# A decoder step on one core: small first loads, one prepared unit ahead and products of ones at the beginning

## The chip, the cores and the metric

The kernel runs on one core of one Trainium2 chip. Its time is the device time of one execution in microseconds (us). Five engines work side by side, each through its own list of instructions in order: TensorE (PE, products and transposes), VectorE (DVE), ScalarE (ACT), GpSimd (POOL) and SyncE (SP, which here only issues DMAs). An instruction waits on semaphores for what it reads, and everything behind it on the same engine waits too.

## The reference

One layer of a hybrid decoder for 256 prompt tokens and 64 sample tokens. The change touches its first stage alone, keys and values of 256 memory tokens:

```python
def mem_kv(mem, g, wk, wv):
    mn = rmsnorm(mem, g)                     # (256, 2048)
    k = (mn @ wk).reshape(b, 256, 4, 512)    # 2048 x 2048 weights
    v = (mn @ wv).reshape(b, 256, 4, 512)
```

Behind it come the mixer (RMSNorm of the tokens, W_in, state space and short convolution, W_out), attention over the memory and a layer of 16384 single-neuron experts, all in float32.

## The kernel before

A float32 product is made of three products in a reduced format: each operand x is split into a high part H (ACT, line 248) and a rest L = x - H (DVE, line 249), and the sum of a-high by H, a-high by L and a-low by H is accumulated.

The stage works in **units**. For each of w_mem_k and w_mem_v and each of four blocks c of 512 columns there are 16 units k, one for each 128 rows of weights: 128 units in all. A unit has a load (one DMA of two units' weights, 512 KB, into one of four rooms `W`), a preparation (`prep`: the split into H and L) and its products (`comp`: six products of 128x512, lines 318 to 320, three for each half of the memory tokens). The units of the first block take their first rooms from `w0`.

The memory rows come as two tiles of 128 tokens x 2048 (`mem`, printed `xt`). The generator `mem_in` makes the stationary operands: one step transposes two 128-column pieces of both tiles on PE (four transposes, line 241, into `pt`), and ACT and DVE scale them by the norm gain and split them into `MH` and `ML` (`scaled_split`, lines 281 and 282), for the units k = 2g and 2g + 1. After eight such steps two more square the rows for the norm's scale (line 459), which is applied when a block leaves PSUM.

`Stream` orders all this at build time. `add` issues a unit's load at once and holds three units back; `prepare` takes the next, emits the preparation of the unit before it (`late`) and puts the new one in a queue; when more than `room["g"]` units (GD = 6) are queued, `pop` emits the oldest one's products. With each pop, side generators advance at their rates: `mem_in` 0.75 steps a unit, and the chain of `x_norm` (norm and transposes of the layer's tokens), `vectors` (norm and convolution weights) and `histories` (convolution states) 0.3. PE, ACT and DVE run in the order that is written; SP and POOL are ordered by a scheduler.

Of the kernel before, what the change touches and what calls it, by code (L numbers as in the profile page):

```python
# [19 lines left out]
P = 128  # L20
# [23 lines left out]
HLB, GD, WA, WB = 7, 6, 3, 4  # L44
# [105 lines left out]
def wait(n):  # L150
    for _ in range(n):
        yield 1
# [11 lines left out]
def step(ctx, tc, ins, outs, dbg=None, stop=None):  # L164
    nc = tc.nc
# [22 lines left out]
    def ps(name="ps"):  # L188
        return psp.tile([P, 512], F32, tag="ps", name=name)

    V, S, G, PE = nc.vector, nc.scalar, nc.gpsimd, nc.tensor
# [6 lines left out]
    ones = cst.tile([P, P], F32, tag="ones", bufs=1, name="ones")  # L198
# [9 lines left out]
    def wtile(beside=None):  # L208

        r = min((r for r in range(len(rooms)) if rooms[r][1] is None),  # L210
                key=lambda r: (rooms[r ^ 1][1] is not beside, rooms[r][2]))
        rooms[r][1] = rooms[r][0]
        return rooms[r][0]
# [12 lines left out]
    def wfree(w):  # L226
        for r in rooms:
            if r[1] is w:
                r[1:] = None, next(turn)
# [3 lines left out]
    def high():  # L233
        return wp.tile([P, 512], F32R, tag="H", bufs=HLB, name="H")

    def low():
        return wp.tile([P, 512], F32R, tag="L", bufs=HLB, name="L")

    def transpose(out, in_):
        n = in_.shape[0]  # L240
        PE.transpose(out, in_, ident[:n, :n])


    strm = Stream(WA, g=GD, a=2)

    def split(h, l, src):

        S.activation(h, src, AF.Copy)  # L248
        V.tensor_tensor(l, src, h.bitcast(F32), ALU.subtract)  # L249
# [37 lines left out]
    def tokens_gemm(w2d, c, ah, al, evac, w0=None):  # L287

        pts, box = [], {}

        def unit(k):
            def load():
                if k % 2 == 0:
                    if w0 is not None and k < 4:
                        w = w0[k // 2]
                    else:
                        w = wtile()
                        nc.sync.dma_start(w.rearrange("p (k n) -> p k n", n=512),
                                          w2d[k * P:(k + 2) * P, 512 * c:512 * c + 512].rearrange("(k p) n -> p k n", p=P))
                    box["room", k + 1] = box["w"] = w  # L300
                box["w", k] = box["w"][:, 512 * (k % 2):512 * (k % 2) + 512]

            def prep():
                h, l = high(), low()
                split(h, l, box.pop(("w", k)))
                if k % 2:
                    wfree(box.pop(("room", k)))
                box[k] = h, l
                if w0 is not None and k == 0:
                    next(mi)  # L310

            def comp():
                if k == 0:
                    pts.extend(ps(f"pg{m}") for m in range(2))
                h, l = box.pop(k)
                for m in range(2):
                    a0, a1 = ah[:, k, m * P:(m + 1) * P], al[:, k, m * P:(m + 1) * P]
                    PE.matmul(pts[m], a0, h, start=k == 0, stop=False)
                    PE.matmul(pts[m], a0, l, start=False, stop=False)
                    PE.matmul(pts[m], a1, h, start=False, stop=k == KC - 1)  # L320
                if k == KC - 1:
                    for m in range(2):
                        evac(m, pts[m])

            strm.add(load, None, prep, comp)

        for k in range(KC):
            unit(k)
# [93 lines left out]
    def norm_T(src, n, gb, h, l, cols):  # L422

        xt = tokens()
        nc.sync.dma_start(xt[:n], src)
        yield from wait(2)
        V.scalar_tensor_tensor(xt[:n], xt[:n], stats(xt, n), gb[:n], ALU.mult, ALU.mult)
        yield from wait(2)
        for g in range(4):
            pt = ps("pt")  # L430
            for j in range(4):
                k = 4 * g + j
                transpose(pt[:, j * n:(j + 1) * n], xt[:n, k * P:(k + 1) * P])
            split(h[:, 4 * g:4 * g + 4, cols], l[:, 4 * g:4 * g + 4, cols],
                  pt[:, 0:4 * n].rearrange("p (j n) -> p j n", j=4))
            yield 1

    def gain_rows(g):
        gb = pM.tile([P, D], F32, tag="gb", bufs=1, name="gb")
        nc.sync.dma_start(gb, g.rearrange("(o d) -> o d", o=1).broadcast_to([P, D]))  # L440
        return gb
# [3 lines left out]
    nc.sync.dma_start(gk, norm_mem_kv[0].rearrange("(k p) -> k p", p=P))  # L445
    mem = [tokens() for _ in range(2)]
    w0 = [wtile()]
    w0.append(wtile(w0[0]))

    for i, (c0, c1) in enumerate(((0, 512), (512, 1024), (1024, 2048))):  # L450
        for b in range(2):
            nc.sync.dma_start(mem[b][:, c0:c1], mem_prompt[0, b * P:(b + 1) * P, c0:c1])
        if i < 2:
            nc.sync.dma_start(w0[i], w_mem_k[0, 256 * i:256 * i + 256, 0:512].rearrange("(k p) n -> p k n", p=P))
    squares = [pM.tile([P, 4], F32, name=f"sq{b}") for b in range(2)]

    def half_square(b, i):
# [2 lines left out]

    S.activation(squares[0][:, 0:1], ones[:, 0:1], AF.Sqrt)
    pk = ps("pk")
    transpose(pk[:, 0:16], gk)
    V.tensor_copy(GAIN[:, 48:64], pk[:, 0:16])
    mem_scale = []

    def mem_in():
        for g in range(8):
            pt = ps("pt")
            for j in range(2):  # L470
                for b in range(2):
                    transpose(pt[:, (2 * j + b) * P:(2 * j + b + 1) * P], mem[b][:, (2 * g + j) * P:(2 * g + j + 1) * P])
            for j in range(2):
                k = 2 * g + j
                scaled_split(MH[:, k], ML[:, k], pt[:, j * TP:(j + 1) * TP], gain(3, k))
            yield 1
        for b in range(2):
            half_square(b, 0)
            half_square(b, 1)
            sq = squares[b]  # L480
            V.tensor_tensor(sq[:, 0:1], sq[:, 0:1], sq[:, 1:2], ALU.add)
            mem_scale.append(rstd(sq, P))
            yield 1

    mi = mem_in()
    next(mi)
    strm.side(mi, 0.75)

    def x_norm():
        gb = gain_rows(norm_mix[0])  # L490
        yield from wait(2)
        for b in range(2):
            yield from norm_T(x_prompt[0, b * P:(b + 1) * P], P, gb, AH, AL, slice(b * P, b * P + P))
        yield from norm_T(x_sample.rearrange("b l d -> (b l) d"), TS, gb, AH, AL, slice(TP, T))
# [77 lines left out]

    strm.steady = chain(wait(136), ordered_rows(0.272))
    side = strm.side(chain(x_norm(), vectors(), histories()), 0.3)
    for w, dst in ((w_mem_k, p_mem_k), (w_mem_v, p_mem_v)):
        d2 = dst[0, 0].rearrange("m h d -> m (h d)")
        for c in range(4):
            def evac(m, pt, c=c, d2=d2):
                o = pM.tile([P, 512], F32, tag="kvo", bufs=2, name="kvo")
                S.activation(o, pt, AF.Copy, scale=mem_scale[m])  # L580
                nc.gpsimd.dma_start(d2[m * P:m * P + P, 512 * c:512 * c + 512], o)
# [1634 lines left out]
```

## Time and profile before

| | us |
|---|---|
| time, median of three runs (lowest, highest) | 3133.64 (3127.72, 3135.29) |
| the profiled execution: its time | 3134.84 |
| the profiled execution: span from first to last instruction | 3133.1 |
| TensorE busy | 3072.1 (98%) |
| VectorE, ScalarE, GpSimd busy | 2281.8, 1594.7, 1343.9 |
| first product of unit 0 starts | 8.80 |
| first product of the next stage (W_in) starts | 206.16 |

Busy time says how long an engine had an instruction in work. The rows by time give the start, the time in work, engine, line, operation, written and read tiles, and in brackets how long the engine sat idle before and what released it. PE's products overlap, so the distance between their starts is their price.

### The profile page before, as it was taken

Reading aid. Unit: us, or ns where it says so; the run is one execution under the profiler, and the core shown is the slowest. Engines: PE = TensorE matmul, PEld = TensorE weight load, DVE = VectorE, ACT = ScalarE, POOL = GpSimd, SP = SyncE. Lnnn points to the kernel's source line nnn. Section 1 sums busy time; section 2 is a strip of 40 time slices with the busy share of each in tenths; the row PEclk is TensorE's granted clock in tenths of the full one; section 3 lists DMA queues with packets and bytes.
Section 4 is the critical chain, followed back from the end, with each engine's and each line's share of the span. In section 5 each row is a group of like instructions: output and inputs, shape, how many; then the busy total and the mean of one; then the engine's idle time right before and its main releaser. Section 6 shows DMA issues by size and latency. Waiting matters only on the chain. (4 is left out here: it accounts for less than half of the span.)

```text
span 3133.1 us, 55416 instructions
## 1 busy us (share of the span) xinstructions
PE 3072.1 (98%) x19749; PEld 2806.7 (90%) x19749; DVE 2281.8 (73%) x4482; ACT 1594.7 (51%) x3207; POOL 1343.9 (43%) x1490
## 2 busy tenths in 40 slices
PE   8999999999999998999999999999999999999997
PEld 7889999999999998779999999888888888878886
DVE  5556766666566456556787899988885888878886
ACT  5545544334554443334454444776675555545555
POOL 0012221111100012320348999989886656456553
PEclk9999999999999999999999999999999999999999
DMA  7668899899999999984866788879998999899996
GB/s 259 210 194 299 307 325 322 308 326 311 335 322 309 314 292 241 252 263 145 228 212 216 274 318 306 314 280 327 329 337 263 340 345 362 314 324 332 327 320 200
DMA packets 442177, 909.15 MB, mean 290 GB/s; under 512 B 39679, under 2 KB 248743, under 8 KB 416388
## 3 DMA queue, kind: packets, MB, share of 16 engines
q1 hardware_dynamic: 313804, 544.07, 51.1%
q0 software_dynamic: 60512, 227.32, 22.3%
q10 hardware_dynamic: 67584, 134.23, 12.4%
q8 instruction: 154, 2.52, 0.3%
q14 instruction: 123, 1.01, 0.1%
HBM read 849.41 MB, written 190.05 MB: 332 GB/s over the span
## 5 line engine op out<-in xcount | busy, mean ns | idle before, releaser
L249 DVE TENSOR_TENSOR L<-W,H 128x512 fp32r<-128x512 f32 x1320 | 903.5, 709 | 390.2 <-ACT H L248 377.3
L248 ACT ACTIVATE H<-W 128x512 fp32r<-128x512 f32 x1320 | 797.4, 625 | 694.9 <-PE acc L2119 216.0
L1924 POOL TENSOR_TENSOR L<-tt,H 128x512 fp32r<-128x512 f32 x509 | 645.0, 1299 | 63.7 <-ACT H L1921 55.9
L371 PE MATMUL pg<-AH,H 128*128 128x320 f32 (+1 forms) x1872 | 587.6, 314 | 0.0
L373 PE MATMUL pg<-AH,L 128*128 128x320 f32 (+1 forms) x1872 | 578.8, 309 | 0.0
L372 PE MATMUL pg<-AL,H 128*128 128x320 f32 (+1 forms) x1872 | 578.4, 309 | 0.0
L2118 PE MATMUL acc<-L,wt 128*128 128x512 f32 x1024 | 399.9, 390 | 4.0 <-DVE L L249 4.0
L2117 PE MATMUL acc<-H,wt 128*128 128x512 f32 x1024 | 399.4, 390 | 2.9 <-DVE at L1957 2.9
L2119 PE MATMUL acc<-H,wt 128*128 128x512 f32 x1024 | 399.5, 390 | 0.0
L1912 DVE STREAM_TRANSPOSE tt<-W 128x512 f32<-128x512 f32 x512 | 337.0, 690 | 59.9 <-POOL L L1924 57.4
L1943 PE MATMUL pu<-XP,H 128*128 128x512 f32 x1050 | 376.8, 399 | 0.0
L1921 ACT ACTIVATE H<-tt 128x512 fp32r<-128x512 f32 x512 | 306.7, 625 | 134.0 <-DVE tt L1912 105.0
L371 PEld LDWEIGHTS pg<-AH,H 128*128 128x128 f32 (+1 forms) x1872 | 350.9, 187 | 2.4 <-issue 0.2
L372 PEld LDWEIGHTS pg<-AL,H 128*128 128x128 f32 (+1 forms) x1872 | 350.6, 187 | 2.2
L373 PEld LDWEIGHTS pg<-AH,L 128*128 128x128 f32 (+1 forms) x1872 | 350.4, 187 | 0.6
L1944 PE MATMUL pu<-XP,L 128*128 128x256 f32 x1120 | 301.5, 279 | 0.1
L2066 POOL TENSOR_TENSOR at<-at,G 128x108 f32<-128x108 f32 x192 | 161.4, 854 | 262.8 <-DMA at<-act_d 228.5
L1950 PE MATMUL pu<-XP,L 128*128 128x256 f32 x928 | 263.8, 284 | 3.7 <-POOL L L1924 3.5
L1948 PE MATMUL pu<-XP,H 128*128 128x256 f32 x928 | 263.2, 284 | 0.0
L1949 PE MATMUL pu<-XP,H 128*128 128x256 f32 x928 | 262.5, 283 | 0.0
L2118 PEld LDWEIGHTS acc<-L,wt 128*128 128x128 f32 x1024 | 192.9, 188 | 45.2 <-DVE L L249 5.0
L1943 PEld LDWEIGHTS pu<-XP,H 128*128 128x128 f32 x1050 | 197.1, 188 | 40.3
(496 smaller groups left out, 5822.0 us busy)
## 6 DMA issues: line engine op xcount, KB each, us to landing
u_d<-in_peer_u_dram ACTq DMA_DIRECT2D x128, 1024.0 KB
W<-u_d SPq DMA_DIRECT2D x128, 1024.0 KB
W<-in_peer_v_dram SPq DMA_DIRECT2D x256, 512.0 KB
W<-in_w_in_dram SPq DMA_DIRECT2D x176, 512.0 KB
W<-in_w_out_dram SPq DMA_DIRECT2D x64, 512.0 KB
W<-in_w_mem_k_dram SPq DMA_DIRECT2D x32, 512.0 KB
W<-in_w_mem_v_dram SPq DMA_DIRECT2D x32, 512.0 KB
W<-in_w_mem_q_dram SPq DMA_DIRECT2D x32, 512.0 KB
```

Source lines behind the costliest of these rows:

```text
L248: S.activation(h, src, AF.Copy)
L249: V.tensor_tensor(l, src, h.bitcast(F32), ALU.subtract)
L371: PE.matmul(out, hv[:, j, c0:c1], ah[:, k, 0:n], start=st, stop=False)
L372: PE.matmul(out, hv[:, j, c0:c1], al[:, k, 0:n], start=False, stop=False)
L373: PE.matmul(out, lv[:, j, c0:c1], ah[:, k, 0:n], start=False, stop=sp)
L1912: V.transpose(tt.rearrange("p (k a i) -> p k a i", a=4, i=32), box["x", i].rearrange("p (a k j) -> p k a j", a=4, k=16)[:, 4 * q:4 * q + 4])
L1921: S.activation(h, src, AF.Copy)
L1924: G.tensor_tensor(l, src, h.bitcast(F32), ALU.subtract)
L1943: PE.matmul(*wide, start=k == 0, stop=False)
L2117: PE.matmul(out, th, h, start=i == 0, stop=False)
L2118: PE.matmul(out, th, l, start=False, stop=False)
L2119: PE.matmul(out, tl, h, start=False, stop=i == P - 1)
```

## The change

The first loads become smaller and alternate: gk, then memory columns 0:256 of both tiles and the weights of units 0 and 1 as two DMAs of 256 KB, then columns 256:768 and units 2 and 3, and so on up to unit 7; all four rooms are `w0` from the start. Until unit 11 has been popped the stream's room is one unit instead of six. `mem_in` is no longer a side generator: its steps are called behind the products of units 0, 2, 4, 6, 8, 10, 11, 13 and 14. Seven products of a tile of ones with itself are put on PE: two before and two after the transpose of gk, three after the first transposes. `x_norm` starts with six more empty steps.

```diff
@@ tokens_gemm
-                    if w0 is not None and k < 4:
+                    if w0 is not None and k < 8:
                         w = w0[k // 2]
...
                 box[k] = h, l
-                if w0 is not None and k == 0:
-                    next(mi)
...
                     PE.matmul(pts[m], a1, h, start=False, stop=k == KC - 1)
+                if w0 is not None:
+                    if k in (0, 2, 4, 6, 8, 10, 11, 13, 14):
+                        next(mi)
+                    if k == 11:
+                        strm.room["g"] = GD
@@ beginning
-    w0.append(wtile(w0[0]))
-
-    for i, (c0, c1) in enumerate(((0, 512), (512, 1024), (1024, 2048))):
+    for i in range(3):
+        w0.append(wtile(w0[-1] if i % 2 == 0 else None))
+
+    for i, (c0, c1) in enumerate(((0, 256), (256, 768), (768, 1408), (1408, 2048))):
         for b in range(2):
             nc.sync.dma_start(mem[b][:, c0:c1], mem_prompt[0, b * P:(b + 1) * P, c0:c1])
-        if i < 2:
-            nc.sync.dma_start(w0[i], w_mem_k[0, 256 * i:256 * i + 256, 0:512].rearrange("(k p) n -> p k n", p=P))
+        for j in range(2):
+            r0 = 256 * i + P * j
+            nc.sync.dma_start(w0[i][:, 512 * j:512 * j + 512], w_mem_k[0, r0:r0 + P, 0:512])
...
+    def warm(n):
+        for _ in range(n):
+            PE.matmul(pk[:, P:2 * P], ones, ones, start=True, stop=True)
+
+    warm(2)
     transpose(pk[:, 0:16], gk)
     V.tensor_copy(GAIN[:, 48:64], pk[:, 0:16])
+    warm(2)
...
     next(mi)
-    strm.side(mi, 0.75)
+    warm(3)
+    strm.room["g"] = 1

     def x_norm():
+        yield from wait(6)
         gb = gain_rows(norm_mix[0])
```

What moves on ACT at the beginning, before (pt_236 is the third group of transposes, H_182 belongs to unit 0, H_195 to unit 1 and so on):

```order
L281 ACTIVATE MH_136<-pt_156,GAIN_77 128x256 x2
L248 ACTIVATE H_182<-W_78 128x512
L281 ACTIVATE MH_136<-pt_186,GAIN_77 128x256 x2
L248 ACTIVATE H_195<-W_78 128x512
L248 ACTIVATE H_200<-W_78 128x512
L248 ACTIVATE H_204<-W_78 128x512
L248 ACTIVATE H_209<-W_78 128x512
L248 ACTIVATE H_213<-W_78 128x512
L248 ACTIVATE H_226<-W_78 128x512
L281 ACTIVATE MH_136<-pt_236,GAIN_77 128x256 x2
L248 ACTIVATE H_245<-W_78 128x512
```

And now (pt_208, pt_237 are the second and third group, H_196 belongs to unit 0, H_217 to unit 1, H_227 to 2, H_246 to 3):

```order
L281 ACTIVATE MH_136<-pt_168,GAIN_77 128x256 x2
L248 ACTIVATE H_196<-W_78 128x512
L281 ACTIVATE MH_136<-pt_208,GAIN_77 128x256 x2
L248 ACTIVATE H_217<-W_78 128x512
L248 ACTIVATE H_227<-W_78 128x512
L281 ACTIVATE MH_136<-pt_237,GAIN_77 128x256 x2
L248 ACTIVATE H_246<-W_78 128x512
L248 ACTIVATE H_257<-W_78 128x512
```

Before, the H of units 1 to 6 stand ahead of the third pair of MH; now each pair of MH stands ahead of the H of the next two units. DVE has the same order with ML and L.

On PE, around the third group of transposes, before:

```order
L318 MATMUL pg1_218<-H_195,MH_136 128x512
L319 MATMUL pg1_218<-L_196,MH_136 128x512
L320 MATMUL pg1_218<-H_195,ML_137 128x512
L241 MATMUL pt_236<-ident_68,xt_140 128x128
L241 MATMUL pt_236<-ident_68,xt_141 128x128
L241 MATMUL pt_236<-ident_68,xt_140 128x128
L241 MATMUL pt_236<-ident_68,xt_141 128x128
L318 MATMUL pg0_217<-H_200,MH_136 128x512
L319 MATMUL pg0_217<-L_201,MH_136 128x512
```

And now:

```order
L316 MATMUL pg1_201<-H_227,MH_136 128x512
L317 MATMUL pg1_201<-L_228,MH_136 128x512
L318 MATMUL pg1_201<-H_227,ML_137 128x512
L241 MATMUL pt_237<-ident_68,xt_140 128x128
L241 MATMUL pt_237<-ident_68,xt_141 128x128
L241 MATMUL pt_237<-ident_68,xt_140 128x128
L241 MATMUL pt_237<-ident_68,xt_141 128x128
L316 MATMUL pg0_200<-H_246,MH_136 128x512
L317 MATMUL pg0_200<-L_247,MH_136 128x512
```

The group moved from behind unit 1 to behind unit 2; the first product behind it reads the H of unit 2 before, which stood ahead of this group's MH on ACT, and the H of unit 3 now, which stands behind it.

## The prediction

> **What bounds the kernel now.** I read the page's engine table, the busy time by stretches, TensorE's waits and the order in time of the first 46 us.
>
> ```profile
> span 3133.1 us, 55416 instructions
> PE 3072.1 (98%) x19749; PEld 2806.7 (90%) x19749; DVE 2281.8 (73%) x4482; ACT 1594.7 (51%) x3207; POOL 1343.9 (43%) x1490
> 0.00:9.00 9.00, 2.68 (x10) 1.92 (x10) 1.48 (x5) 3.31 (x6) 3.78 (x16) 1.00 0.76 203
> 9.00:15.00 6.00, 6.00 (x19) 4.47 (x20) 3.34 (x6) 2.26 (x5) 0.40 (x2) 1.00 0.96 369
> 15.00:30.00 15.00, 15.00 (x77) 12.16 (x76) 10.78 (x20) 9.47 (x21) 0.00 (x0) 1.00 0.75 282
> 30.00:45.40 15.40, 13.01 (x47) 9.45 (x46) 9.36 (x31) 14.22 (x27) 1.09 (x2) 0.89 0.78 266
> 45.40:100.00 54.60, 54.60 (x252) 44.89 (x251) 34.59 (x54) 29.45 (x51) 2.17 (x4) 1.00 0.72 231
> ```
>
> TensorE is busy 98% of the span. In the stretches (PE, PEld, DVE, ACT, POOL busy, then granted clock) it has no idle time from 45.4 to 100 us and, at 98% of the whole, little later, so whatever shifts the product stream by 45 us shifts the end by as much. What is to be won lies before: 6.3 us without products up to 9 us, 2.4 us idle in 30 to 45.4, and slow products. The clock column says 1.00 from 9 to 15 us, yet the rows there say otherwise:
>
> ```profile
> 12.26 0.63 PE L319 MATMUL pg<-L,MH 128*128 128x512 f32 x1
> 12.69 0.63 PE L320 MATMUL pg<-H,ML 128*128 128x512 f32 x1
> ...
> 13.54 0.40 PE L319 MATMUL pg<-L,MH 128*128 128x512 f32 x1
> 13.78 0.39 PE L320 MATMUL pg<-H,ML 128*128 128x512 f32 x1
> 14.01 0.60 PE L241 MATMUL pt<-ident,xt 128*128 128x128 f32 x4
> 14.36 0.48 PE L318 MATMUL pg<-H,MH 128*128 128x512 f32 x1
> 14.68 0.40 PE L319 MATMUL pg<-L,MH 128*128 128x512 f32 x1
> 14.92 0.39 PE L320 MATMUL pg<-H,ML 128*128 128x512 f32 x1
> ```
>
> Up to 13.5 us products start 0.43 us apart, later 0.23: half clock, then full. A unit's six products take 6 x 0.229 = 1.37 us at full clock, 2.57 at half. A block of four transposes adds (14.68 - 13.78) - 2 x 0.23 = 0.44.
>
> ```profile
> 35.97 0.50 PE L319 MATMUL pg<-L,MH 128*128 128x512 f32 x1 [0.55 <-DVE L L249]
> ...
> 37.02 0.40 PE L320 MATMUL pg<-H,ML 128*128 128x512 f32 x1
> 38.28 0.50 PE L318 MATMUL pg<-H,MH 128*128 128x512 f32 x1 [0.87 <-ACT H L248]
> 39.76 0.50 PE L319 MATMUL pg<-L,MH 128*128 128x512 f32 x1 [0.98 <-DVE L L249]
> 40.80 0.57 PE L320 MATMUL pg<-H,ML 128*128 128x512 f32 x1
> 41.17 0.63 PE L318 MATMUL pg<-H,MH 128*128 128x512 f32 x1
> ...
> 44.15 0.45 PE L319 MATMUL pg<-L,MH 128*128 128x512 f32 x1
> ...
> 45.14 0.40 PE L320 MATMUL pg<-H,ML 128*128 128x512 f32 x1
> ```
>
> The second lesson: after two pauses of 0.87 and 0.98 us the clock halves at 40.8 and comes back at 44.15, 3.4 us later. Counting six products a unit, the last row is the last product of unit 18, whose slot ends at **45.37**. That is the mark I compare with.
>
> TensorE's waits in the first 46 us, by what it waited for (us in total, times, longest):
>
> ```profile
> PE pk L241 <- DMA gk<-in_norm_mem_kv_dram: 2.7, 1, 2.7
> PE pg L318 <- ACT H L248: 2.7, 2, 1.8
> PE pg L319 <- DVE L L249: 1.5, 2, 1.0
> ```
>
> The last two are the first product's wait and the pauses at 35 to 40 us.
>
> **The change, part by part.** *The chain from a transpose block to a product* is what the sum rests on:
>
> ```profile
> 5.26 1.76 PE L241 MATMUL pt<-ident,xt 128*128 128x128 f32 x7 [0.32 <-DMA xt<-in_mem_prompt_dram]
> 6.20 0.47 ACT L281 ACTIVATE MH<-pt,GAIN 128x256 fp32r<-128x256 f32 x1 [3.88 <-PE pt L241]
> 6.71 0.48 DVE L282 SCALAR_TENSOR_TENSOR ML<-pt,GAIN,MH 128x256 fp32r<-128x256 f32 x1 [3.58 <-ACT MH L281]
> 7.23 0.47 ACT L281 ACTIVATE MH<-pt,GAIN 128x256 fp32r<-128x256 f32 x1 [0.55 <-DVE ML L282]
> 7.74 0.48 DVE L282 SCALAR_TENSOR_TENSOR ML<-pt,GAIN,MH 128x256 fp32r<-128x256 f32 x1 [0.54 <-ACT MH L281]
> 8.12 0.63 ACT L248 ACTIVATE H<-W 128x512 fp32r<-128x512 f32 x1 [0.42 <-DMA W<-in_w_mem_k_dram]
> 8.78 0.69 DVE L249 TENSOR_TENSOR L<-W,H 128x512 fp32r<-128x512 f32 x1 [0.44 <-ACT H L248]
> 8.80 0.80 PE L318 MATMUL pg<-H,MH 128*128 128x512 f32 x1 [1.79 <-ACT H L248]
> 9.53 0.80 PE L319 MATMUL pg<-L,MH 128*128 128x512 f32 x1
> ```
>
> ACT's second MH waits for DVE's first ML (0.55 idle), so MH, ML, MH take 7.70 - 6.20 = 1.5 us; H takes 0.63 and the product follows 0.05 after it: 2.2 us from first MH to first product without the 0.42 for the weights. The second product needs L and stands 0.73 behind the first, in place of 0.23.
>
> Before, this chain is paid once, since six H lie on ACT ahead of the third MH pair. The room of one takes that lead away. A unit is split only when the next is prepared, and its products are popped at once, so on every engine the order becomes: split of k, products of k. The hand-placed steps put transposes and MH/ML after units 0, 2, 4, 6, 8, 10 and 11. As the order of the change shows, after each block the next unit's H stands behind that block's MH pair on ACT, its L behind the ML pair on DVE, and its products directly behind the block on PE. Nothing on PE covers the chain. One round costs
>
> - last transpose's start to first MH: the fourth transpose of the first group starts near 5.26 + 2 x 0.21 = 5.69, so 0.5 us; I take 0.45 for both clocks;
> - first MH to first product 2.2;
> - the wait for L, 0.73 - 0.23 = 0.5;
> - less the transpose's own slot, 0.1: **3.05 us**, seven times: 21.4.
>
> *Start.* The first memory pieces go from 256 to 128 KB each, and in front of the first weights stand 256 KB instead of 512. The two first pieces arrive 0.8 us apart (waits ending at 4.47 and 5.26):
>
> ```profile
> 4.47 0.48 PE L241 MATMUL pt<-ident,xt 128*128 128x128 f32 x1 [1.55 <-DMA xt<-in_mem_prompt_dram]
> ```
>
> Half the bytes should take 0.4 off the second and at most as much off the first, and the wait of 0.42 for weights goes. I put the first product at 7.6 instead of 8.80 (bounds 7.2 and 8.8).
>
> *Products of ones.* Seven, priced by the nearest row, ones against 128 columns:
>
> ```profile
> L675 PE MATMUL ptc<-ones,AN 128*32 128x128 f32 x2 | 0.6, 421 | 0.0
> ```
>
> 2.9 us at that price, under 5 if the clock is halved. Four stand before or around the wait for gk, three behind the first block, under its 2.2 us of MH, ML, MH, H: nothing. Without that cover, up to 1.9 us. They cannot keep the clock up through rounds that pause for 3 us.
>
> *SP.* Six more issues and the earlier gain rows and norm vectors:
>
> ```profile
> 28.62 0.42 SPq L522 DMA_DIRECT2D vecs<-in_norm_final_dram  x1
> ```
>
> Eight vector loads of some 0.45 us lie between the weights of units 8 and 10: 3.6 us of SP. Unit 10 is six rounds away, over 25 us, so that is covered: 0. `x_norm` comes 6 / 0.3 = 20 units later, about 27 us of products; what it makes is read only behind unit 127. The state histories move with it, behind units 120, 123 and 126. Their three loads wait on the same buffer and stand as many products apart as before, when they cost
>
> ```profile
> 170.69 1.14 PE L241 MATMUL pth<-ident,hx 24*128 24x24 f32 x16 [0.73 <-DMA hx<-in_state_ssd_conv_dram]
> ```
>
> so 0, bounded by 0 and 1.5 us (two such waits), the first wide weights of the next stage being issued about 6 us before the stage ends.
>
> *Squares of the memory rows.* They caused the pauses at 34.9 to 39.8. In the change the lead of six is back at unit 11, seven H lie ahead of the squares, and PE has 1.37 us of products for each: that stall goes. It is contained in the mark.
>
> *Sum at full clock.* First product 7.6; units 0 to 18, 19 x 1.37 = 26.1; seven blocks, 3.1; seven rounds, 21.4: unit 18 ends at 58.2, against 45.37: **+12.8**.
>
> *The clock.* Each round idles 3.05 us around one product. Before, 1.85 us of pause within the 3.4 us ahead of 40.8 brought 3.4 us of half clock; those hold 8 products, each 0.2 longer: 1.6 us. Part of a slow stretch will fall into the next pause, so I take 1.4 a round: +9.8. Bounds: nothing; or half clock all through, 13 units x 6 x 0.2 + 7 x 0.5 = 19 us.
>
> Together +22.6 us. The profiled execution took 3134.84 us (span 3133.1), 1.2 above the median of 3133.64; 3134.8 + 22.6 - 1.2 = **3156**.
>
> The Trainium skill (TensorE: Matmul & The Clock Gate, HAM oscillation) puts it as a rule that no idle gap between products should exceed about 3.4 us if the clock is to stay up. The pauses here are 2.6 and 0.5 us, so by that rule the sum would be the +12.8 alone. The trace disagrees with the rule taken gap by gap (0.87 and 0.98 us were enough), while its slow stretch of 3.4 us agrees with the length of the window that the page gives.
>
> **The rivals.**
> *Clock holds.* Seven rounds of 3.05 us at full clock: 3134.8 + 12.8 - 1.2 = 3146. For it: no single pause is longer than 2.6 us; the pause of 0.55 us at 35.97 alone left it up (0.40 for the product at 37.02). Against: the drop at 40.8. This is the page's rule as a mechanism.
> *Half clock throughout.* 3134.8 + 12.8 + 19 - 1.2 = 3165. For it: every stretch of 3.4 us may catch most of a pause, and a half-clock round keeps no long busy run. Against: the return at 13.54 and 44.15 after 4 us of steady products, about what a round holds.
> *Not slower.* The chain is covered after all: H of the next unit is there when its products come up, as "one unit ahead" says. Then 1.2 us at the start, 12 slow products x 0.2 = 2.4 and about 4 of the squares' stall and its slow clock are won: 3134.8 - 7.6 - 1.2 = 3126. It decides at 7.6 / 7 = 1.1 us a round. For it: PE is busy from 9 to 30 without a pause (6.00 of 6.00 and 15.00 of 15.00) with transposes between its products. Against: that rested on six H in front; in the new order H stands behind the MH pair.
>
> **How the numbers follow.** Likeliest, 3156 (range of its own 3150 to 3163): 0.63. Clock holds 0.13, half clock throughout 0.12, not slower 0.10, something outside 0.02. From 3143 to 3167 the first three are held, 0.88. This kernel's measurement can tell some 0.3%, 9.4 us, from no change. Even the full-clock sum is beyond that: slower 0.88; the not-slower case ends at 0.24%, thus same 0.10; faster 0.02.
>
> **What would show it.** In the changed profile: PE idle in front of L316 after each block, about 2.6 us, ended by ACT H, then 0.5 us in front of L317 ended by DVE L, each seven times; PE's waits for H and L in all near 20 us, against 2.7 + 1.5 in these rows; the first product near 7.6; products 0.43 apart behind the pauses; no pauses at the squares; no shift after 70 us. The forecast is wrong if PE waits for ACT H less than a microsecond per block, if weights arrive late at units 8 to 12, or if the state histories stall the end of the stage.

## The result, and the profile after

The change takes 3157.2 us (median of six runs, 3151.1 to 3159.5) against 3134.2 before (six runs, 3126.1 to 3139.2); the ratio is 1.0076, 95% interval 1.0061 to 1.0091: slower by 23 us. The profiled execution took 3157.21 us. The page of the changed kernel, and its busy time by stretches (PE, PEld, DVE, ACT, POOL busy with instruction counts, then granted clock, DMA share, GB/s; PEld is TensorE's loading of stationary operands), cut at the first product and at the end of unit 18:

```profile
span 3155.4 us, 55456 instructions
PE 3086.0 (98%) x19763; PEld 2814.1 (89%) x19763; DVE 2279.3 (72%) x4482; ACT 1595.8 (51%) x3207; POOL 1352.3 (43%) x1490
0.00:7.35 7.35, 4.84 (x20) 4.10 (x20) 1.20 (x5) 2.95 (x5) 3.77 (x16) 1.00 0.61 157
7.35:67.23 59.88, 44.01 (x142) 31.89 (x143) 22.38 (x51) 23.66 (x48) 1.24 (x4) 0.89 0.50 174
67.23:228.00 160.77, 160.77 (x748) 129.89 (x747) 87.31 (x150) 84.11 (x150) 6.71 (x13) 1.00 0.64 208
```

The same cuts of the kernel before:

```profile
8.80:45.37 36.57, 34.17 (x138) 26.26 (x139) 23.65 (x57) 26.15 (x52) 1.49 (x4) 0.95 0.80 289
45.37:206.16 160.79, 160.06 (x748) 129.81 (x746) 86.14 (x143) 82.61 (x147) 6.50 (x12) 1.00 0.64 203
```

From first product to the end of unit 18 it was 36.6 us and is 59.9, of which PE is busy 44.0. Behind unit 18 both take 160.8 us to the end of the stage with the same 748 products and transposes. The lag is 67.23 - 45.37 = 21.9 us at unit 18, 228.0 - 206.2 = 21.8 at the end of the stage and 3155.4 - 3133.1 = 22.3 at the end: it arises in the first 67 us, and nothing behind gives it back.

One round in order of time, around the fifth block of transposes:

```profile
34.13 0.40 PE L318 MATMUL pg<-H,ML 128*128 128x512 f32 x1
34.37 0.60 PE L241 MATMUL pt<-ident,xt 128*128 128x128 f32 x4
35.00 0.47 ACT L281 ACTIVATE MH<-pt,GAIN 128x256 fp32r<-128x256 f32 x1 [4.83 <-PE pt L241]
35.51 0.48 DVE L282 SCALAR_TENSOR_TENSOR ML<-pt,GAIN,MH 128x256 fp32r<-128x256 f32 x1 [4.53 <-ACT MH L281]
36.03 0.47 ACT L281 ACTIVATE MH<-pt,GAIN 128x256 fp32r<-128x256 f32 x1 [0.55 <-DVE ML L282]
36.40 1.14 ACT L248 ACTIVATE H<-W 128x512 fp32r<-128x512 f32 x2
37.05 1.29 DVE L249 TENSOR_TENSOR L<-W,H 128x512 fp32r<-128x512 f32 x2
37.07 0.51 PE L316 MATMUL pg<-H,MH 128*128 128x512 f32 x1 [2.11 <-ACT H L248]
37.80 0.50 PE L317 MATMUL pg<-L,MH 128*128 128x512 f32 x1 [0.22 <-DVE L L249]
```

ACT had been idle 4.83 us before the first MH: it waits for PE's transposes, and PE then waits for ACT. The H of the next two units follow the MH pair, as the order said. PE's waits in the first 80 us (us in total, times, longest):

```profile
PE pg L316 <- ACT H L248: 15.6, 8, 2.1
PE pg L317 <- DVE L L249: 1.1, 5, 0.2
```

One of the eight, 0.83 us, stands before the first product; the other seven are the rounds.

### The profile page after: what moved, and what is told of

The parts are those of the page before. It is cut to its first block, busy times and chain, and to the rows that moved or that the text cites. A ratio compares the mean times of both kernels' runs of the same rounds, so it can differ in the third digit from the quotient of the medians.

```text
span 3155.4 us, 55456 instructions
## 1 busy us (share of the span) xinstructions
PE 3086.0 (98%) x19763; PEld 2814.1 (89%) x19763; DVE 2279.3 (72%) x4482; ACT 1595.8 (51%) x3207; POOL 1352.3 (43%) x1490
## 4 chain that ended last, share of the span: by engine, by line
PE 32%; DMA 9%; DVE 3%; issue 3%; POOL 2%; ACT 1%; DVEq 0%; POOLq 0%; SPq 0%; ACTq 0%
PE pu L1957 7%; DMA gv<-in_peer_v_dram,EV 4%; PE pu L1958 4%; DMA at<-act_d 3%; PE acc L2132 3%; PE acc L2133 3%; PE acc L2131 3%; PE pu L1964 3%; PE pu L1963 3%; PE pu L1962 3%; PE pgate L1860 2%; DVE L L249 1%; POOL L L1938 1%; DMA W<-in_peer_v_dram 1%; POOL at L2080 1%
```

## The experiments

The common measure is the end of unit 18, from one profile of each kernel. The time of the whole spreads by 7 to 23 us between runs of one kernel, so a difference of a few us shows in it only over many runs. Each ratio is against runs of the kernel before from the same occasion, whose medians lie between 3127.8 and 3134.2 us. Where an expectation says 67.0 for the change, that is its last product's start; its slot ends at 67.23.

| kernel | first product | end of unit 18 | ratio to before (95%) |
|---|---|---|---|
| before | 8.80 | 45.37 | |
| the change, room one | 7.35 | 67.23 | 1.0076 (1.0061 to 1.0091) |
| room two | 7.39 | 48.12 | 1.0015 (0.9999 to 1.0032) |
| room three | 7.40 | 39.88 | 0.9995 (0.9983 to 1.0006) |
| room six | 7.39 | 43.24 | 1.0007 (0.9993 to 1.0021) |
| before with room one alone | 8.57 | 66.67 | 1.0076 (1.0059 to 1.0092) |
| the change without ones | 7.24 | 65.94 | 1.0076 (1.0059 to 1.0093) |
| the change, pauses filled | 7.39 | 58.91 | 1.0064 (1.0044 to 1.0085) |
| before with the loads alone | 9.77 | 42.46 | 1.0005 (0.9990 to 1.0021) |
| room three, eleven ones | 7.63 | 38.04 | 0.9987 (0.9974 to 1.0000) |
| the same again | 7.62 | 37.95 | 0.9977 (0.9963 to 0.9991) |

**Room six**: the change with its smaller room undone.

```diff
-                    if k == 11:
-                        strm.room["g"] = GD
...
-    strm.room["g"] = 1
```

> The change with one part undone: the stream's room stays at six units from the start; small loads, products of ones, the hand-placed steps and the later norm stay. Theory (the room of one puts each unit's H behind the MH pair): the seven pauses of about 2.4 us in front of L316 go, only the first block may wait about 1 us because MH stands behind six H that wait for weights; unit 18 ends near 41 us instead of 67.0, and the time is about 3130 us (before 3134.2, change 3157.2). Rival (small loads, SP's order or the later norm cause the loss): unit 18 stays beyond 60 us and the time above 3150.

The seven pauses are gone, so neither the small loads nor the placed steps nor the later norm cause the loss. Unit 18 ends at 43.2, 2 us later than expected, since the one pause, behind the first of the seven blocks, was larger than I thought. The order in time of this kernel shows why:

```profile
11.46 0.40 PE L318 MATMUL pg<-H,ML 128*128 128x512 f32 x1
13.44 1.30 ACT L248 ACTIVATE H<-W 128x512 fp32r<-128x512 f32 x2 [1.59 <-DMA W<-in_w_mem_k_dram]
14.66 0.46 ACT L281 ACTIVATE MH<-pt,GAIN 128x256 fp32r<-128x256 f32 x1
15.16 0.50 PE L316 MATMUL pg<-H,MH 128*128 128x512 f32 x1 [3.31 <-ACT MH L281]
```

With six H in front, MH stands behind weights that land at 13.4 us; PE waits 3.3 us for it. Behind this pause the clock halves too: the products stand 0.43 us apart from 16.9 to 19.9 us.

**Room one alone**, in the kernel before.

```diff
+                if w0 is not None and k == 11:
+                    strm.room["g"] = GD
...
     strm.side(mi, 0.75)
+    strm.room["g"] = 1
```

> The kernel before with one part of the change alone: room of one until unit 11's products; loads, side rate of 0.75, norm as before, no products of ones. Theory: six blocks of transposes each followed by a pause of about 2.4 us plus 0.5, the squares cost about 3.5 us more, and the clock halves in between: unit 18 ends near 70 us, the time is about 3158 us. Rival (the room alone is harmless, the loads or the placed steps do it): 3134 to 3137, unit 18 near 46.

```profile
PE pg L318 <- ACT H L248: 13.9, 7, 2.1
PE pg L319 <- DVE L L249: 2.0, 6, 0.5
```

Six rounds with the same wait of 2.1 us (the seventh wait, 1.26 us, is the first product's), and the whole loss: 66.67 and 1.0076. The room alone is enough; everything else in the change is not needed for it. Unit 18 came 3 us earlier than the 70 expected, because the squares cost 0.7 us there and not 3.5.

**Room two and room three**: one number of the change, 2 or 3 in place of 1.

> The change with room for two units until unit 11: one unit's products (1.37 us at full clock, 2.57 at half) cover part of the chain of about 2.7 us. Theory (dose and response): pauses of about 1.2 us, one per block, none where the clock is still halved; unit 18 ends at 45 to 50 us, time about 3 us above or below before. Rival (any small room costs the same): pauses of 2.4 us and unit 18 beyond 60.

> The change with room for three units until unit 11 instead of one: three H stand ahead of each MH pair, so two units' products cover the chain of 2.7 us, and the second MH pair no longer waits behind six weights as in the kernel with room six (3.7 us there). Theory: no pause above 1 us after the first product at 7.4, no pause at the squares, unit 18 ends at 39 to 41 us against 45.4 before; time 4 to 6 us below before, ratio near 0.998. Rival (the steps placed by hand, not the room, limit the stage): pauses stay at every second unit, unit 18 beyond 50.

With room two, one unit's products lie between a block and the first H behind it:

```profile
25.00 0.60 PE L241 MATMUL pt<-ident,xt 128*128 128x128 f32 x4
25.36 0.48 PE L316 MATMUL pg<-H,MH 128*128 128x512 f32 x1
...
26.60 0.40 PE L318 MATMUL pg<-H,ML 128*128 128x512 f32 x1
27.71 0.51 PE L316 MATMUL pg<-H,MH 128*128 128x512 f32 x1 [0.72 <-ACT H L248]
```

From the block's start to the product that waits it is 2.71 us here (25.00 to 27.71), as in room one (34.36, where the product's slot ends, to 37.07). But room one has only the block, 0.44, under it, and room two has the 1.37 us of one unit as well: the pause is 0.88 us (1.11 between starts, less 0.23). With room three the pauses are gone:

```profile
7.40:39.88 32.48, 32.29 (x142) 25.97 (x143) 20.63 (x42) 20.93 (x42) 0.38 (x2) 1.00 0.82 295
```

PE is busy 32.29 of 32.48 us. 67.2, 48.1, 39.9, then 43.2 again with six: by these marks three is the best of the four, between a chain that nothing covers and MH behind weights not yet landed. The clock has little part in the differences from two to six: products stand 0.43 us apart up to 12.6 us with room two, up to 12.9 with three, and for a few products less, each 0.2 us longer, from 16.9 to 19.9 with six. The times don't tell two, three and six apart, since their intervals overlap, and the 4 to 6 us below before expected of room three aren't shown: its interval, 0.9983 to 1.0006, holds no change as well.

**Pauses filled**: products of ones behind each block.

```diff
+FILL = {0: 5, 2: 5, 4: 9, 6: 9, 8: 9, 10: 9, 11: 9}
...
+                    if k in (0, 2, 4, 6, 8, 10, 11):
+                        pw = ps("pw")
+                        for _ in range(FILL[k]):
+                            PE.matmul(pw[:, 0:P], ones, ones, start=True, stop=True)
```

> The change with products of ones written behind each of the seven blocks of transposes (5, 5, then 9 each, into a bank of their own that nothing reads), to keep TensorE active in the pauses without shortening them. Theory (about 10 us of the 22 are the half clock that the pauses bring): products behind the pauses start 0.23 us apart, unit 18 ends near 58 us instead of 67.0, the time is about 3149 us. Rival (the pauses themselves are all of the loss, or ones do not count as activity): unit 18 stays at 66 to 69 us, 3157.

```profile
20.00:59.00 39.00, 37.15 (x207) 30.41 (x207) 17.54 (x42) 18.50 (x38) 0.00 (x0) 1.00 0.38 127
```

The rounds are as long as in the change (23.04 to 25.74 us, 2.70), the clock stays at 1.00, and unit 18 ends 8.3 us earlier. Half clock was that much of the 21.9 us; the rest is the pauses, less what the change saves elsewhere. In the times these 8.3 us aren't shown: the intervals of 1.0064 and 1.0076 overlap.

**Without ones**: the three calls of `warm` taken out.

> The change without the seven products of ones at the beginning. Theory: they are hidden and bring nothing: first product at 7.35 us as in the change, unit 18 within 2 us of 67.0 (the clock's phase may shift), time as in the change, 3157. Rival (they keep the clock from being worse, or they delay the start): unit 18 more than 3 us later, or the first product more than 0.3 us earlier.

The seven ones neither help nor harm by much: without them the first product is 0.1 us earlier and unit 18 ends 1.3 us earlier.

**The loads alone**, in the kernel before.

> The kernel before with the small alternating loads alone. Theory: first product near 7.4 instead of 8.8 us, then the order of before with its stall at the squares; unit 18 ends near 44 against 45.4; time not distinguishable from before (ratio 0.999 to 1.001). Rival (eight more issues on SP starve later units): waits for weights at units 4 to 10 that reach PE, unit 18 beyond 47.

The expectation missed the start. There the second block of transposes precedes unit 0's products, and it reads columns 256 to 511, which now come with the second piece:

```profile
8.56 0.48 PE L241 MATMUL pt<-ident,xt 128*128 128x128 f32 x1 [3.42 <-DMA xt<-in_mem_prompt_dram]
9.77 0.78 PE L318 MATMUL pg<-H,MH 128*128 128x512 f32 x1
```

The small pieces start products earlier only with a block order that reads them in turn, which the change has. Unit 18 still ends 2.9 us earlier than before; the time isn't distinguishable.

**Room three with eleven ones** (3, 3 and 5, into a bank of their own, so that none waits for the copy of the gain).

> Room three and eleven products of ones instead of seven (3, 3, 5, into a bank of their own, so that none waits for the copy of the gain), which keep PE busy from 1.2 us to the first product. Theory: the clock is at full speed by the first product or soon after, products 0.23 us apart from unit 0 or 1; unit 18 ends at 37 to 39 us, ratio near 0.997. Rival (ones and transposes do not raise the clock, or the clock's window starts too late): products 0.43 apart until about 14 us and unit 18 as with room three alone.

> The kernel of room three with eleven products of ones once more, on another occasion, because its interval reached just to 1. If the 7.3 us won by unit 18 last to the end, the ratio is near 0.9977 and the interval lies below 1; unit 18 ends at 37 to 41 us, by where the clock's window falls. Rival (what is won at the beginning is lost in the spread of the later stages): an interval around 1.

```profile
7.63 0.50 PE L316 MATMUL pg<-H,MH 128*128 128x512 f32 x1 [0.32 <-ACT H L248]
8.36 0.51 PE L317 MATMUL pg<-L,MH 128*128 128x512 f32 x1 [0.22 <-DVE L L249]
8.70 0.40 PE L318 MATMUL pg<-H,ML 128*128 128x512 f32 x1
8.93 0.40 PE L316 MATMUL pg<-H,MH 128*128 128x512 f32 x1
```

Products stand 0.23 us apart from unit 0 on in both profiles, and unit 18 ends at 38.0, 7.3 us earlier than before. The second set of runs has an interval below 1; 0.9977 of 3130.8 is 7.2 us. This version is faster than the kernel before by 0.2% in the second set, while the first set's interval reaches 1; both sets lie below the change.

## Why the prediction was right, point by point

- **The chain and the round.** Right in kind, 10% too long. At full clock 34.36 to 37.07 is 2.71, plus 0.73 - 0.23 for L, less 0.44 for the block: 2.77 us a round against 3.05, seven times 19.4 against 21.4. Two terms were too large: the block's slots end at 34.80 and the first MH starts at 35.00, 0.20 later, where I took 0.45 - 0.1; and first MH to first product is 37.07 - 35.00 = 2.07 where I took 2.2.
- **Idle time in the rows.** I expected 2.6 and 0.5 us in front of L316 and L317, near 20 in all; the rows say 2.11 and 0.22, 16.7 in all with the first product's 0.83. The idle time of a row begins at the modelled end of the transposes, so starts of products, not idle times, are to be compared.
- **Start.** 7.35 against 7.6. I put the ones at nothing; without them the first product comes 0.11 us earlier.
- **The clock.** +9.8 forecast. What is left of 67.23 after 7.35, 26.1 of products, 3.1 of blocks and 19.4 of rounds is 11.3; filling the pauses gave back 8.3. That pauses halve the clock was right, but that the size came near is in part luck. I took 1.4 us for each of seven rounds; in the rows half clock lasts from the first product to 19.39 us and comes back in four stretches of 3.41 us, from 22.80, 29.62, 43.28 and 56.92. My sum has no term for the slow start, which the kernel before also has, up to 13.5 us. The rival in which the clock holds is refuted by the rows below, the one with half clock throughout too: only some rounds bring it.
- **Squares, SP, later norm, histories.** No pause at the squares: from 57 us on PE has 0.23 to 0.43 between starts. From unit 18 to the end of the stage it takes 160.77 us without a pause against 160.79 before, so the nine vector loads, the later norm and the histories cost nothing. The 0.7 us wait of the histories before is gone, but the stage isn't shorter for it.
- **The sum.** Errors of -0.25, -2 and +1.5 nearly cancelled, which is luck: unit 18 at 67.2 where the terms gave 68.0, time 3157.2 against 3156. The full-clock rival (3146) lies below every run, the not-slower one (the chain is covered) by the waits of 2.1 us in each round, which the room alone brings.

## What to carry to other kernels

Before shortening a queue, write down each engine's order around one hand-over: if the consumer's next operand stands behind work that waits for the consumer itself, the two engines take turns, and each round costs the whole chain. A depth is best chosen from two numbers, the chain's length over the cover of one unit (2.7 us over 1.37, so two units of products, which a room of three leaves), and the landing time of the weights that then stand in front. And a pause on TensorE is paid twice where it also halves the clock.

## What the runs showed of the hardware

The clock of the changed kernel, cut at moments at which it changes, 3.41 us apart:

```profile
19.39:22.80 3.41, 1.07 (x6) 0.53 (x4) 1.73 (x4) 1.99 (x4) 0.00 (x0) 1.00 0.28 93
22.80:26.21 3.41, 3.41 (x9) 2.66 (x10) 0.53 (x1) 0.00 (x0) 0.00 (x0) 0.53 0.52 161
26.21:29.62 3.41, 1.40 (x8) 0.98 (x6) 0.93 (x2) 1.43 (x4) 0.00 (x0) 0.97 0.00 0
29.62:33.04 3.42, 3.31 (x7) 2.33 (x8) 1.33 (x3) 0.56 (x2) 0.00 (x0) 0.53 0.36 122
33.04:36.45 3.41, 1.93 (x10) 1.32 (x9) 0.48 (x1) 0.90 (x3) 0.00 (x0) 0.97 0.08 31
36.45:39.86 3.41, 2.57 (x10) 1.91 (x11) 1.78 (x3) 1.09 (x3) 0.00 (x0) 1.00 0.27 69
39.86:43.28 3.42, 1.31 (x9) 0.90 (x7) 1.12 (x3) 1.65 (x4) 0.00 (x0) 1.00 0.25 89
43.28:46.69 3.41, 3.22 (x8) 2.29 (x9) 1.14 (x2) 0.33 (x1) 0.00 (x0) 0.53 0.47 147
46.69:50.10 3.41, 1.81 (x10) 1.30 (x8) 0.51 (x2) 1.01 (x3) 0.00 (x0) 0.97 0.02 7
50.10:53.50 3.40, 2.36 (x10) 1.54 (x10) 1.15 (x2) 0.72 (x2) 0.00 (x0) 1.00 0.26 76
```

And of the kernel before, around its one slow stretch:

```profile
37.43:40.85 3.42, 1.59 (x6) 1.09 (x7) 2.67 (x10) 3.34 (x8) 0.00 (x0) 1.00 0.80 249
40.85:44.26 3.41, 3.41 (x10) 2.67 (x9) 2.02 (x5) 3.19 (x7) 1.09 (x2) 0.50 1.01 378
```

Half clock follows a full-clock stretch with PE busy 1.07, 1.40, 1.31 or 1.59 of 3.41 us, and doesn't follow 1.81, 1.93, 2.36 or 2.57: in these rows it is the busy share of a fixed stretch of 3.41 us, with the line between 47% and 53%, not the length of a pause, that decides. A pause of the same length costs the clock or not, by where it falls. That is why rounds differ, and why I had to guess the share. The Trainium skill (TensorE: Matmul & The Clock Gate, Part 1) gives a free-running window of 3413 ns, whose length these rows bear out. Its rule that gaps stay under about 3.4 us (HAM oscillation) was not enough here: behind the first product every pause of these two kernels is under 2.8 us. That the half-clock stretches follow from the busy share is read from these profiles; no run varied the share by itself, apart from the filled pauses, which kept the clock at 1.00.

That line is for the fall. Coming back took more, as the kernel before with room one alone shows:

```profile
23.12:26.54 3.42, 3.10 (x9) 2.12 (x9) 0.00 (x0) 0.28 (x1) 0.00 (x0) 0.51 0.44 153
26.54:29.95 3.41, 1.40 (x5) 0.95 (x6) 2.26 (x4) 1.70 (x4) 0.00 (x0) 0.99 0.00 0
...
43.62:47.03 3.41, 1.81 (x7) 1.11 (x5) 0.51 (x2) 1.01 (x3) 0.00 (x0) 0.51 0.43 154
47.03:50.45 3.42, 2.91 (x6) 2.09 (x7) 1.91 (x5) 3.16 (x6) 0.00 (x0) 0.50 0.11 31
50.45:53.86 3.41, 3.41 (x9) 2.65 (x9) 1.78 (x9) 2.91 (x6) 0.00 (x0) 0.50 0.92 318
53.86:57.27 3.41, 2.87 (x12) 2.01 (x12) 3.00 (x10) 3.28 (x8) 0.00 (x0) 0.99 0.96 368
```

At half clock 1.81 and 2.91 us busy left it at half, and 3.10 and 3.41 brought full clock back, as 3.41, 3.31 and 3.22 did in the change: in these rows the line is between 85% and 91%.

Second, the beginning of the change on the same grid:

```profile
2.33:5.74 3.41, 2.95 (x14) 2.68 (x14) 0.17 (x1) 0.46 (x1) 2.10 (x6) 1.00 0.85 224
5.74:9.16 3.42, 2.59 (x8) 1.66 (x8) 1.69 (x4) 1.00 (x3) 0.00 (x0) 1.00 0.93 276
```

The column says 1.00 here, but the products stand 0.43 us apart from 8.66 us on, so this is half clock. The seven ones with their gaps, 2.95 and 2.59 us busy, were too little by the line above. With eleven ones, which leave hardly a gap, PE was at full speed at 7.6 us in both profiles; with seven it was in one of the kernels (room six) and not in the change, room two, room three and the filled one. How much of that is where the stretches fall isn't shown by so few profiles.
